# Turning attention probabilities on VectorE and moving them inside SBUF, in place of TensorE transposes

## The chip, the cores and the metric

The kernel runs on one core of a Trainium2 chip. The metric is the device time of one execution in microseconds. Engines are named TensorE (PE in the profile, with its weight loads as PEld), VectorE (DVE), ScalarE (ACT), GpSimd (POOL) and SyncE (SP), which issues DMA transfers. SBUF has 128 partitions; PSUM has eight banks of 512 float32 columns on each.

## The reference

One layer of a hybrid decoder over 4096 new tokens (and a small batch of 64 sample tokens), model width 1024, all in float32:

```
h = rmsnorm(x) ; z = h @ w_in                       # one projection, split among three head groups
A: silu(g) * B * conv3(C * h)                       # gated short convolution, 256 channels
B: window attention, 128 keys back, 8 query heads on 2 key heads, width 64,
   softmax with one learned sink logit per head, in blocks of 128 queries, * silu(g)
C: attention of 4 heads into 256 memory tokens, softmax, * silu(g)
y = concat(A, B, C) @ w_out ; out = x + rmsnorm(y)
```

For one block of 128 queries, B has 8 matrices of probabilities (queries x the 128 live keys: each query sees keys of its own block up to itself and keys of the block before beyond itself, so 128 columns hold both parts), and C has 4 heads x 2 halves of 128 memory keys. To multiply probabilities by values, TensorE needs them with the keys on the partitions; the softmax leaves them with the queries there.

## The kernel before, in words

**The projection** (`input_projection`) comes first, about 950 us. It multiplies blocks of 520 tokens in three phases, by a scheme of seven products, and stores queries, keys (`qd`), values (`vd`, transposed: features by tokens) and gates (`md`) in DRAM. Its third phase also runs small jobs (`third_jobs`), among them the memory keys and the whole attention of groups 0 and 1 (`early_scores`, `early_transposes`, `early_values`), the first 256 tokens.

**The attention stage** goes over 32 blocks of 128 tokens, `blocks[i]`, and a block of sample tokens near the end. `Block.run` makes the output product of block i: two halves of 512 columns, y0 and y1 (`p` 0 and 1), each 24 matmuls (8 slices x 3 passes of a float32 split into parts `mh` and `ml`). Between the slices it calls what `events_of(i)` has put at (half, slice):

- at (0, 0) `values_and_scores(i)`: scores of group i+3 (`scores`: window scores into four PSUM banks, memory scores into two), values of group i+1 (`values`: probabilities times values, into one two-bank PSUM tile `pv`, then two gate products on VectorE, `cross_gate` and the one at the end of `values`, in place in `mix`), and the softmax of group i+3;
- also there, the load `xr` of block i+2's residual input; at (0, 1) in even blocks `chunk_load`, keys and queries of a chunk of two blocks, issued by GpSimd; in odd blocks `load_mix`, 1 MB of gates;
- at (1, 0) `transposes(i)`: eight window matrices (`band_transposes`, TensorE into PSUM, copied out by ScalarE, masked twice per half by GpSimd's `affine_select` into `pv` and `pt`) and eight memory matrices (`cross_transposes`, copied out by VectorE and ScalarE); in even blocks also two transposes of the chunk's values (`Chunk.values`);
- at (1, 3) `split` of block i+1: ScalarE's cast `mh`, VectorE's difference `ml`.

After each half VectorE scales it (`yn`) and ScalarE squares and sums it; after both, the norm factor `yst` (VectorE, then a power on GpSimd), VectorE's product with the residual (`xr`), and the store `o_yp`, issued by SyncE. In the softmax, ScalarE copies the live half of the scores to SBUF, VectorE puts the other block's keys in their place (`copy_predicated`), takes the maximum, and ScalarE does eight exponentials with their sums; VectorE divides. The memory softmax reads PSUM, and GpSimd divides.

**What sets the order.** Every engine runs its own queue in order. In the projection's first two phases the order is the program's (`manual_schedule`). In the attention stage a planner orders the queues by its own cost estimates, apart from instructions marked `keep_in_program_order`. SyncE's transfers take eight semaphores in turn; a transfer waits until the one eight before it has landed. `yn` has one buffer, `xr` two: the load of a block's `xr` waits until the store of the block two before it has landed. `sm` and `xp`, the probabilities, have one buffer for odd groups and share three for even ones. Output halves lie in PSUM banks 0 and 5.

Of the kernel before, what the change touches and what calls it, by code (L numbers as in the profile page):

```python
# [51 lines left out]
def hybrid_layer(ctx: ExitStack, tc: tile.TileContext, a: dict):  # L52
    nc = tc.nc
    TE, V, S, G, DMA = nc.tensor, nc.vector, nc.scalar, nc.gpsimd, nc.sync
# [26 lines left out]
    vd = tc.dram_tile([P, NT], F32, name="vd")  # L81
    md = tc.dram_tile([KT, P, NT], F32, name="md")
# [711 lines left out]
    def third_jobs(b, p):  # L794
# [19 lines left out]
        if n > 13 and third["chunk"]:  # L814
            jobs.append(third["chunk"].pop(0))
        elif n > 13 and len(chunks) == 1:
            jobs.append(lambda: (chunk_load(1), chunks[1].load_values()))
        elif n > 13 and early[0] < 4 and n >= 38:
            if early[0] == 0:
                groups[2] = Group(chunks[1], 0)  # L820
            jobs.append(lambda u=early[0]: groups[2].early_scores(u))
            early[0] += 1
        return jobs

    early = [0]

    def first_chunk():
# [5 lines left out]
        chunk.load_values()  # L833
        chunk.load_mix()
        third["chunk"] = [lambda: chunk.values(None)]
# [66 lines left out]
    def input_projection():  # L902
        for i, (ph, b, p) in enumerate(steps):
# [36 lines left out]
            if ph == 2 and b == last:  # L940
# [4 lines left out]
                if p == 6:  # L945
                    jobs.append(blocks[0].split)
# [35 lines left out]
    def open_attention():  # L982
# [7 lines left out]
        vp = ctx.enter_context(tc.tile_pool(name="vp", bufs=5, side="right"))  # L990
# [40 lines left out]
    class Chunk:  # L1031
# [19 lines left out]
        def load_values(self):  # L1051

            self.vT = self.pool().tile([P, CT], F32, tag="vT", name=f"vT{self.c}")
            DMA.dma_start(self.vT, vd[:, self.ts])

# [14 lines left out]
        def values(self, vt_prev, pv=None):  # L1070

            self.vts = [vt_prev]
            ts = [psum(0, f"vtp{self.c}_{i}")[:, 0:P] if pv is None else pv[:, P * i : P * i + P] for i in range(2)]
            for i in range(2):
                TE.transpose(ts[i], self.vT[:, i * P : i * P + P], ident)
            for i in range(2):
                if self.c == 0:
                    vt = third["vt"] if i else third["work"].tile([P, P], F32, tag="v", name="vt0_0", bufs=1)
                else:
                    vt = vp.tile([P, P], F32, tag="v", name=f"vt{self.c}_{i}")  # L1080
                S.mul(vt, ts[i], 0.5)
                self.vts.append(vt)

    class Group:


        def __init__(self, chunk, i):
            self.chunk, self.i, self.b = chunk, i, 2 * chunk.c + i
            self.pt, self.pv, self.xpt = {}, {}, {}

        def open_scores(self, n):
            b = self.b
            if n == 0:
                t = wp.tile([P, D], F32, tag="sm", name=f"sm{b}", bufs=1) if b % 2 and b > 1 else work(f"sm{b}")
                self.sm = t.rearrange("p (h k) -> p h k", h=8)
            if n == 3:
                t = wp.tile([P, D], F32, tag="p", name=f"xp{b}", bufs=1) if b % 2 and b > 1 else work(f"xp{b}")
                self.p = t.rearrange("p (h j k) -> p h j k", h=2, j=2)

        def early_scores(self, n):  # L1100
# [3 lines left out]
            elif n == 2:  # L1104
                self.band_softmax()
            else:
                self.crosses([psum(0, f"xs{self.b}_{u}").rearrange("p (j k) -> p j k", j=2) for u in range(2)])

        def scores(self):
# [4 lines left out]
            self.bands(bands[:2], 0)  # L1114
            self.bands(bands[2:], 1)
            self.crosses(cross)

# [14 lines left out]
        def crosses(self, banks):  # L1132
            for j in range(2):
                self.both_rows([banks[u][:, j] for u in range(2)], self.chunk.q[:, j, :, self.i * P : self.i * P + P], third["mk"][:, :, j])
            for u in range(2):
                self.cross_softmax(banks[u], u)

        def band_out(self, s3, half, kvh):
            to = self.sm[:, 4 * kvh + 2 * half : 4 * kvh + 2 * half + 2, :]
            S.copy(to, s3[:, :, P : 2 * P])  # L1140
            V.copy_predicated(to, third["wmask"], third["negs"].unsqueeze(2).to_broadcast([P, 2, P]) if self.b == 0 else s3[:, :, 0:P])  # L1141

        def band_softmax(self):
# [3 lines left out]
            V.tensor_reduce(mx, sm, axis=AX.X, op=ALU.max)  # L1147
            V.scalar_tensor_tensor(nm, mx, -SCALE, third["nsink"], op0=ALU.mult, op1=ALU.min)  # L1148
            V.tensor_tensor(es, nm, third["sink"], op=ALU.add)
            S.activation(es, es, AF.Exp)  # L1150
            for h in range(n):
                S.activation(sm[:, h, :], sm[:, h, :], AF.Exp, bias=nm[:, h : h + 1], scale=SCALE, accum_out=den[:, h : h + 1])  # L1152
            V.tensor_tensor(den, den, es, op=ALU.add)  # L1153
            V.reciprocal(rd, den)
            V.tensor_tensor(sm, sm, rd.unsqueeze(2).to_broadcast([P, n, P]), op=ALU.mult)

        def cross_softmax(self, s, hh):
            p = self.p[:, hh]
# [490 lines left out]
```

## Time and profile before

| | us |
|---|---|
| median of 3 runs | 1551.4 (1550.34 to 1551.58) |
| the profiled execution | 1549.0 |
| its span, first to last instruction | 1547.3 |
| TensorE busy | 1525.7 |
| VectorE busy | 1124.6 |
| ScalarE busy | 776.8 |
| GpSimd busy | 335.6 |

The profile is one execution. A page gives busy times and the chain of work that ended last; queries give windows (busy time of every engine in a stretch), groups (instructions of one line with count, busy time, mean, and the idle time before them), the timeline, and waits. Matmuls are pipelined, so the time a matmul costs is the distance to the next one's start. SyncE has no busy time; its rows show when a transfer was issued and how long the issue took. In a TensorE row, `wt<-ident,sm` reads: wt is written, from ident and sm.

### The profile page before, as it was taken

The numbers are of one execution on the slowest core, as the hardware profiler recorded it, in microseconds if no ns is written. First come the engines' busy times: TensorE is split into PE (matmuls) and PEld (weight loads), VectorE is DVE, ScalarE is ACT, GpSimd is POOL, SyncE is SP. The second block draws the span as 40 slices with busy tenths as digits, with TensorE's granted clock in tenths as the row PEclk, the third lists the DMA queues.
The fourth block names the chain that finished last, engine by engine and source line by source line (L and its number), as shares of the span: only waits on it lengthen the run. The fifth ranks groups of instructions, "written<-read, shape, count | busy, mean of one in ns | idle before, by whom it ended". The sixth has DMA issues, their size and how long they took to land.

```text
span 1547.3 us, 30906 instructions
## 1 busy us (share of the span) xinstructions
PE 1525.7 (99%) x11981; PEld 1400.8 (91%) x11981; DVE 1124.6 (73%) x1850; ACT 776.8 (50%) x1964; POOL 335.6 (22%) x522
## 2 busy tenths in 40 slices
PE   9999999999999999999999998999999999999998
PEld 9999999999999999999999997788888888888776
DVE  6779888897988777996776678566666666666654
ACT  6776566475222222344454445555555555555541
POOL 0323323220400000000000101343333434334320
PEclk9999999999999999999999999999999999999999
DMA  9979999877755333669666859744554544445432
GB/s 260 212 204 257 262 274 266 276 243 269 198 179 179 125 125 126 215 209 304 234 216 199 255 189 299 219 145 137 143 161 147 150 137 137 137 137 160 153 107 96
DMA packets 169735, 299.47 MB, mean 194 GB/s; under 512 B 29813, under 2 KB 99445, under 8 KB 169557
## 3 DMA queue, kind: packets, MB, share of 16 engines
q1 hardware_dynamic: 128069, 226.69, 46.1%
q0 software_dynamic: 40800, 69.76, 16.9%
q8 instruction: 94, 1.54, 0.4%
q10 hardware_dynamic: 720, 1.05, 0.2%
q14 instruction: 52, 0.43, 0.1%
HBM read 190.38 MB, written 108.05 MB: 193 GB/s over the span
## 4 chain that ended last, share of the span: by engine, by line
PE 88%; DVE 4%; issue 3%; DMA 2%; ACT 2%; POOL 1%; SPq 0%; DVEq 0%; POOLq 0%; ACTq 0%
PE c L359 49%; PE y L1471 24%; PE pv L1017 5%; PE ws L1017 3%; PE xt L1207 2%; PE xs L1017 2%; PE wt L1194 2%; PE mem_acc L775 1%; DMA wor<-in_w_out 1%; ACT sm L1152 1%; DMA vd<-v 1%; DVE z L366 0%; DMA wr_2A<-in_w_in 0%; DVE wo L182 0%; POOL md L163 0%
## 5 line engine op out<-in xcount | busy, mean ns | idle before, releaser
L1471 PE MATMUL y<-wo,mh 128*128 128x512 f32 (+1 forms) x1040 | 338.6, 396 | 4.6 <-ACT y L1479 3.3
L366 DVE TENSOR_TENSOR z<-c,z 128x520 f32<-128x520 f32 (+1 forms) x308 | 194.7, 645 | 96.8 <-PE c L359 95.7
L1471 PEld LDWEIGHTS y<-wo,mh 128*128 128x128 f32 x1040 | 195.5, 189 | 56.3 <-DVE sm L1141 10.8
L1471 PE MATMUL y<-wo,ml 128*128 128x512 f32 (+1 forms) x520 | 202.5, 390 | 2.7 <-DVE ml L1450 2.7
L1471 PEld LDWEIGHTS y<-wo,ml 128*128 128x128 f32 x520 | 98.5, 189 | 20.8 <-DVE ml L1450 3.0
L1163 ACT ACTIVATE xp<-xs,xnm 128x256 f32<-128x256 f32 x128 | 59.5, 471 | 115.0 <-DVE xnm L1161 101.8
L1479 ACT ACTIVATE y<-y 128x512 f32<-128x512 f32 (+1 forms) x66 | 38.2, 578 | 130.8 <-DVE yn L1478 130.8
L1167 POOL TENSOR_SCALAR xp<-xp,xrd 128x256 f32<-128x256 f32 x128 | 61.5, 491 | 181.8 <-DVE xnm L1161 111.9
L1152 ACT ACTIVATE sm<-sm,wnm 128x128 f32<-128x128 f32 x256 | 99.1, 388 | 3.0 <-DVE wnm L1148 3.0
L1199 POOL TENSOR_SCALAR_AFFINE_SELECT wpv<-wpt 128x512 f32<-128x512 f32 x62 | 62.4, 1018 | 115.5 <-ACT wpt L1195 109.8
L1153 DVE TENSOR_TENSOR wden<-wden,wes 128x8 f32<-128x8 f32 x32 | 5.3, 167 | 88.3 <-ACT sm L1152 88.3
L1478 DVE TENSOR_TENSOR yn<-y,gpost 128x512 f32<-128x512 f32 (+1 forms) x66 | 45.1, 684 | 27.1 <-PE y L1471 26.4
L1017 PEld LDWEIGHTS ws<-kst,q 64*128 64x128 f32 x768 | 48.3, 188 | 11.3 <-issue 10.5
L734 POOL MEMSET negs<- 128x1 f32 x1 | 0.1, 98 | 264.4 <-PE c L359 264.4
L1017 PE MATMUL ws<-kst,q 64*128 64x256 f32 x768 | 55.4, 290 | 0.0
L368 ACT COPY z<-c 128x520 f32<-128x520 f32 (+1 forms) x44 | 24.4, 554 | 55.5 <-PE c L359 52.9
L1201 POOL TENSOR_SCALAR_AFFINE_SELECT wpt<-wpt 128x512 f32<-128x512 f32 x64 | 40.3, 639 | 52.7 <-ACT wpt L1195 50.5
L1141 DVE COPY_PREDICATED sm<-wmask,ws 128x256 f32<-128x256 uint8 x124 | 48.0, 441 | 4.5 <-ACT sm L1140 3.2
L1485 POOL TENSOR_TENSOR yst<-yst,mhalf 128x1 f32<-128x1 f32 (+1 forms) x33 | 18.4, 557 | 151.0 <-DVE yst L1484 151.0
L1489 DVE SCALAR_TENSOR_TENSOR xr<-yn,yst,xr 128x1024 f32<-128x1024 f32 (+2 forms) x34 | 42.5, 1253 | 8.1 <-POOL yst L1485 8.1
L400 ACT CAST zh<-z 128x520 fp32r<-128x520 f32 x56 | 33.4, 624 | 29.7 <-DVE z L366 26.9
L1152 ACT ACTIVATION_READ_ACCUMULATOR sm<-sm,wnm 128x1 f32 x256 | 48.2, 188 | 0.0
(957 smaller groups left out, 5064.1 us busy)
## 6 DMA issues: line engine op xcount, KB each, us to landing
q<-qd POOLq DMA_DIRECT2D x32, 768.0 KB, 8.5
xr<-in_x_p SPq DMA_DIRECT2D x32, 512.0 KB
nat<-in_x_p SPq DMA_DIRECT2D x39, 416.0 KB
o_yp<-xr SPq DMA_DIRECT2D x31, 512.0 KB
md<-th POOLq DMA_DIRECT2D x48, 260.0 KB, 6.6
qd<-zh SPq DMA_DIRECT2D x48, 260.0 KB
qd<-z SPq DMA_DIRECT2D x48, 260.0 KB
place<-md SPq DMA_DIRECT2D x8, 1024.0 KB
```

The lines of the kernel that those rows point to most:

```text
L359: TE.matmul(bank[:, :HW], l, r, start=first and i == 0, stop=last and i == 3 * KH - 1)
L366: add = lambda dst, other: V.tensor_tensor(dst, c, other, op=ALU.add)
L1017: ins = TE.matmul(o, w, x, **kw)
L1141: V.copy_predicated(to, third["wmask"], third["negs"].unsqueeze(2).to_broadcast([P, 2, P]) if self.b == 0 else s3[:, :, 0:P])
L1152: S.activation(sm[:, h, :], sm[:, h, :], AF.Exp, bias=nm[:, h : h + 1], scale=SCALE, accum_out=den[:, h : h + 1])
L1163: S.activation(p[:, i, :], s[:, i, :], AF.Exp, bias=nm[:, i : i + 1], scale=SCALE, accum_out=den[:, i : i + 1])
L1167: G.tensor_scalar(p[:, i, :], p[:, i, :], rd[:, i : i + 1], 0.5, op0=ALU.mult, op1=ALU.mult)
L1199: G.affine_select(self.pv[u].rearrange("p (h q) -> p h q", h=4), p3, pattern=[[0, 4], [-1, P]], compare_op=ALU.is_gt, fill=0.0, base=0, ch ...
L1201: G.affine_select(p3, p3, pattern=[[0, 4], [1, P]], compare_op=ALU.is_ge, fill=0.0, base=0, channel_multiplier=-1)
L1471: TE.matmul(acc, self.hl[l][:, k], wo[k][c0 // 512][:, r, c0 % 512 : c0 % 512 + c1 - c0], start=j == 0, stop=j == passes * KT - 1)
L1478: V.tensor_tensor(yn[:m, c0:c1], acc[:m], gpost[:m, c0:c1], op=ALU.mult)
L1489: V.scalar_tensor_tensor(self.xr[:m, cs], yn[:m, cs], st[:m, 3:4], self.xr[:m, cs], op0=ALU.mult, op1=ALU.add)
```

## The change

It replaces TensorE's transposes of groups 2 to 31 and of the values of chunks 1 to 15.

1. *Layout.* The probabilities of a group lie as four stripes of 32 keys: `sm` as (stripe, head, 32), `xp` as (stripe, head, half, 32). Masked copies, exponentials and divisions write and read through that order. The factor 0.5 of the gate, which the values carried, goes into the window weights (one more small VectorE product).
2. *Turning.* VectorE transposes each 32x32 square of the 128x1024 tile in place (`V.transpose`). Then sixteen transfers issued by SyncE, each 32 partitions by 1 KB, bring the squares of each stripe to their keys' partitions in a second tile (`wt`, `xt`): 32 transfers a group.
3. *Masks.* Four `affine_select` on GpSimd, now on tiles laid out as (query square, head, 32), two into a second tile `wd`.
4. *Values.* In the projection's third phase eight loads, eight VectorE transposes and 32 stores put the values into DRAM with tokens as rows (`vn`); each block then loads its 128 rows (`half_load`).
5. *The output.* y1 now lies in the second bank of the `pv` tile. Its square, the norm factor, the residual product and the store (`scale`, `store`) run in the next block, between its score matmuls (`tail(0)`, `tail(1)`).
6. *VectorE's order.* In blocks 1 to 30 every VectorE instruction keeps the program's order (`InOrder`). The softmax of a group is cut into maxima (before `values`) and weights (after).
7. The turning of group i+3 stands at (1, 2) of block i, its masks at (0, 4) of block i+1, its values at block i+2. Block 0 does the turning of group 2 at its start.

```
+    class InOrder:
+        on = False
+        def __getattr__(self, name):
+            fn = getattr(nc.vector, name)
+            return (lambda *args, **kw: tc.keep_in_program_order(fn(*args, **kw))) if self.on else fn
+    V = InOrder()
...
+    def v_turn(k):
+        turned = temp(f"vq{k}")[:, :512]
+        V.transpose(turned, third.pop(("v", k)))
+        rows_of = vn[512 * k : 512 * k + 512, :].rearrange("(b i) d -> i b d", i=32)
+        for g in range(4):
+            ds = slice(32 * g, 32 * g + 32)
+            DMA.dma_start(rows_of[:, :, ds], turned[ds].rearrange("p (b j) -> p b j", j=32))
...
+    def half_load(n):
+        halves[n] = vp.tile([P, P], F32, tag="v", name=f"vh{n}")
+        DMA.dma_start(halves[n], vn[P * n : P * n + P, :])
...
             self.bands(bands[:2], 0)
+            tail(0)
             self.bands(bands[2:], 1)
+            tail(1)
             self.crosses(cross)
+            self.band_softmax()
...
-        def transposes(self):
-            for u in range(2):
-                self.pt[u], self.pv[u] = (wp.tile([P, 512], F32, tag=t, name=f"w{t}{self.b}_{u}") for t in ("pt", "pv"))
-                self.band_transposes(u, psum(1 + u, f"wt{self.b}_{u}"))
-            for u in range(2):
-                self.xpt[u] = wp.tile([P, 512], F32, tag="xpt", name=f"xpt{self.b}_{u}")
-                self.cross_transposes(u, psum(3 + u, f"xt{self.b}_{u}"))
+        def moved(self, squares, name):
+            tc.keep_in_program_order(V.transpose(squares, squares))
+            to = wp.tile([P, 4, 256], F32, tag=name, name=f"{name}{self.b}")
+            src = squares.rearrange("p (k n) -> p k n", k=4)
+            for g in range(4):
+                for k in range(4):
+                    DMA.dma_start(to[32 * k : 32 * k + 32, g], src[32 * g : 32 * g + 32, k])
+            return to
+        def masks(self):
+            w = self.w
+            self.wd = wp.tile([P, 2, 8, 32], F32, tag="wd", name=f"wd{self.b}")
...
+            keep(self.wd, w[:, 2:4], P, -1, 64, ALU.is_gt)
+            keep(self.wd[:64], w[:64, 0:2], 64, 1, 0, ALU.is_ge)
+            keep(w[:, 0:2], w[:, 0:2], P, -1, 0, ALU.is_gt)
+            keep(w[:, 2:4], w[:, 2:4], P, 1, 64, ALU.is_ge)
...
         if 2 <= i + 1 < 2 * NCH:
             groups.pop(i + 1).values()
         if g < 2 * NCH:
-            groups[g].band_softmax()
+            for u in range(2):
+                groups[g].cross_softmax(cross[u], u)
+            groups[g].band_weights()
+            for u in range(2):
+                groups[g].cross_weights(u)
...
-                    acc = psum((0, 5, 1)[p], f"y{b}_{p}")[:, : c1 - c0]
+                    acc = (values_psum(f"y{b}_1")[:, 1] if p == 1 else psum(p // 2, f"y{b}_{p}"))[:, : c1 - c0]
...
-        at(1, 0 if i else 2, transposes, i)
+        if i == 0:
+            at(0, 4, turn, 1, 2)
+        at(0, 4, turn, 2, i + 2)
+        if i > 0 and i + 3 < 2 * NCH:
+            at(0, 5, half_load, i + 3)
+        at(1, 2, turn, 0, i + 3)
+        at(1, 2, turn, 1, i + 3)
...
+        InOrder.on = 0 < i < 31
```

More of the change, by code (lines that the diff above doesn't have):

```diff
@@ L1261, in values_and_scores @@
         g = i + 3
-        if g < 2 * NCH:
+        if i == 0:
+            turn(0, 2)
+        if g >= 2 * NCH:
+            tail(0)
+            tail(1)
+        else:
             groups[g] = Group(chunks[g // 2], g % 2)
-            groups[g].scores()
+            cross = groups[g].scores()
         if 2 <= i + 1 < 2 * NCH:
@@ L1497, in hybrid_layer @@
     chunk_load(2)
-    chunks[2].load_values()
+    for n in range(1, 4):
+        half_load(n)
     blocks[0].load()
```

173 lines of the change are left out of this document (108 added, 65 removed).

## The prediction, before the run

> **What bounds the kernel now.** I read the page first (busy shares, then the chain that ended last), then the table of windows, then the timeline of one block of the attention stage, SyncE's timeline over ten blocks, and the groups of VectorE and GpSimd in those blocks.
>
> ```profile
> span 1547.3 us, 30906 instructions
> PE 1525.7 (99%) x11981; PEld 1400.8 (91%) x11981; DVE 1124.6 (73%) x1850; ACT 776.8 (50%) x1964; POOL 335.6 (22%) x522
> PE 88%; DVE 4%; issue 3%; DMA 2%; ACT 2%; POOL 1%; SPq 0%; DVEq 0%; POOLq 0%; ACTq 0%
> ```
>
> TensorE is busy 99% of the span and carries 88% of the chain. So work taken from TensorE shortens the kernel, as long as nothing else takes its place.
>
> ```profile
> 1105.13:1285.30 180.17, 180.17 (x1334) 146.85 (x1332) 115.06 (x241) 102.41 (x380) 69.43 (x106) 1.00 0.50 147
> ```
>
> This window (columns: TensorE, its weight loads, VectorE, ScalarE, GpSimd, clock, DMA share, GB/s) runs from one output store to the tenth after it: ten blocks in 180.17 us, 18.02 us a block. TensorE has no gap; VectorE is busy 11.5 us a block, ScalarE 10.2, GpSimd 6.9, and the DMA engines half the time.
>
> **What is taken from TensorE.** One even block in the timeline, its value matmuls (the first row) and its turning:
>
> ```profile
> 1103.85 1.09 PE L1017 MATMUL pv<-xpt,mv 128*64 128x128 f32 x16
> ...
> 1106.33 0.50 PE L1471 MATMUL y<-wo,mh 128*128 128x512 f32 x1
> ...
> 1111.47 0.39 PE L1471 MATMUL y<-wo,ml 128*128 128x512 f32 x1
> 1111.70 0.39 PE L1471 MATMUL y<-wo,mh 128*128 128x512 f32 x1
> 1111.93 0.38 PE L1075 MATMUL vtp<-ident,vT 128*128 128x128 f32 x2
> 1112.14 1.04 PE L1194 MATMUL wt<-ident,sm 128*128 128x128 f32 x8
> 1113.02 1.04 PE L1207 MATMUL xt<-ident,xp 128*128 128x128 f32 x8
> 1113.81 0.48 PE L1471 MATMUL y<-wo,mh 128*128 128x512 f32 x1
> ```
>
> The matmuls are pipelined, so a price is a distance between starts: all value matmuls into pv 2.5 us (1103.85 to 1106.33), an output matmul 0.23 (1111.47 to 1111.70), the two value transposes 0.21, the eight window transposes 0.88, the eight memory transposes 0.79.
>
> ```profile
> L1194 PE MATMUL wt<-ident,sm x256: 271/273/300, 799.7 to 1496.5; 128*128 128x128 f32 x128
> ```
>
> ```profile
> L1207 PE MATMUL xt<-ident,xp x256: 271/273/328, 820.7 to 1497.7; 128*128 128x128 f32 x128
> ```
>
> ```profile
> L1075 PE MATMUL vtp<-ident,vT x32: 270/272/274, 779.7 to 1475.9; 128*128 128x128 f32 x32
> ```
>
> Of 32 groups, 30 lose their sixteen transposes (groups 0 and 1 keep them), and 15 of 16 chunks lose two: 30 x 1.67 + 15 x 0.21 = 53.3 us. A block would fall from 18.02 to 16.24 us.
>
> **What TensorE gets in exchange.** The second output half y1 now lies in the second bank of the one pv tile. In the built order of the odd blocks from 5 to 27, and of blocks 1 and 4, TensorE runs all 24 matmuls of the first half, then the value matmuls into pv, then y1 at once. y1 must wait until VectorE has read pv by its two gate products. In most even blocks six matmuls of the first half (6 x 0.23 = 1.4 us) stand between and cover that.
>
> ```profile
> L1160 DVE TENSOR_REDUCE xmx<-xs 128x2 f32<-128x512 f32 x20 | 12.8, 681 | 0.0
> L1155 DVE TENSOR_TENSOR sm<-sm,wrd 128x1024 f32<-128x1024 f32 x10 | 12.2, 1224 | 0.3
> L1147 DVE TENSOR_REDUCE wmx<-sm 128x8 f32<-128x1024 f32 x10 | 12.1, 1211 | 0.0
> L1208 DVE COPY xpt<-xt 128x512 f32<-128x512 f32 x10 | 6.8, 680 | 0.0
> L1450 DVE TENSOR_TENSOR ml<-mix,mh 128x1024 fp32r<-128x1024 f32 x5 | 6.1, 1226 | 9.2 <-ACT mh L1447 9.2
> ...
> L1254 DVE TENSOR_TENSOR place<-place,pv 128x512 f32<-128x512 f32 x5 | 3.4, 682 | 0.0
> ...
> L1219 DVE TENSOR_TENSOR place<-place,pv 128x256 f32<-128x256 f32 x5 | 2.1, 414 | 0.0
> ```
>
> The gates take 0.41 + 0.68 = 1.1 us, rounded up to 1.2 for the signals between the engines: 14 blocks with 1.2 us of TensorE idle and block 3, with two matmuls between, some 0.7: 17.5 us back. The value matmuls now read their moving operand in runs of 32 columns, where the window ones read runs of 64 before; I take no change. The other end, a value matmul twice as dear, would cost 2.5 us a block and the whole gain.
>
> **VectorE.** A transpose of 128x1024 is not in the trace. The passes over 1024 columns cost 1.21 to 1.23 us, a product, a maximum or a subtraction; I take 1.22, and for the upper end twice that, as if the squares went through twice. Per block VectorE loses the xpt copy (0.68) and gains two transposes (2.44) and a small product (0.15, an estimate from the small rows): 11.5 - 0.7 + 2.6 = 13.4 us of a block of about 17. It fits, but its order is now fixed in blocks 1 to 30, so each of its waits holds everything behind it. The order runs: yn of y1; four masked copies and the output scaling; the 1.2 us maximum; the gates (wait for pv); the memory maxima; the window weights (wait for eight exponentials); yn of y0; both transposes (the second waits for GpSimd's scaling); ml; yn of y1. From the end of pv to yn of y0 the rows add to 0.41 + 0.68 + 2 x 0.68 + 1.22 + 0.68 (yn, 512 columns like the xpt copy) and about 1.2 of small ones, 5.5 us; the square after it frees the bank of the next scores about 6.3 us after pv. TensorE gets there 5.5 + 1.2 us after pv in an odd block (24 x 0.23, and the wait for the gates), 6.9 in an even one. The slack is 0.4 to 0.6 us. ml ends some 2 us into the next block, where y0 wants it 2.5 us in. With joints this tight I add 0.2 us a block, 29 x 0.2 = 6 us (between 0 and 0.5 a block).
>
> ScalarE only loses work (the copies out of wt, xt and vtp). GpSimd keeps four selections of 512 columns a group:
>
> ```profile
> L1199 POOL TENSOR_SCALAR_AFFINE_SELECT wpv<-wpt 128x512 f32<-128x512 f32 x20 | 21.0, 1060 | 30.5 <-ACT wpt L1195 30.5
> ```
>
> ```profile
> L1201 POOL TENSOR_SCALAR_AFFINE_SELECT wpt<-wpt 128x512 f32<-128x512 f32 x20 | 12.4, 632 | 0.7
> ```
>
> Two at 1.06 and two at 0.63 are 3.4 us. For even groups they stand behind the scaling's power of the odd block (about 4.5 us in) and end near 7.9; the window products start near 9. Nothing is lost; if the masks slipped by over a microsecond, TensorE would pay what is over.
>
> **SyncE and the moves.** Each group adds 32 transfers of 32 rows by 1 KB. Their issues, and what else stands in SyncE's queue:
>
> ```profile
> 1105.13 0.34 SPq L1490 DMA_DIRECT2D o_yp<-xr  x1
> 1111.41 0.33 SPq L1433 DMA_DIRECT2D xr<-in_x_p  x1
> 1112.34 0.32 SPq L1054 DMA_DIRECT2D vT<-vd  x1
> 1119.34 0.37 SPq L1068 DMA_DIRECT2D place<-md  x1
> 1123.30 0.34 SPq L1490 DMA_DIRECT2D o_yp<-xr  x1
> 1127.09 0.33 SPq L1433 DMA_DIRECT2D xr<-in_x_p  x1
> ```
>
> ```profile
> 842.00 0.32 SPq L165 DMA_DIRECT2D qd<-z  x1
> 842.37 0.44 SPq L165 DMA_DIRECT2D qd<-zh  x1
> ```
>
> ```profile
> 1511.95 0.54 SPq L1433 DMA_DIRECT2D xr<-in_x_s  x1
> ```
>
> ```profile
> SPq L1433 <- DMA o_yp<-xr: 100.6, 24, 7.4
> ```
>
> An issue costs 0.31 to 0.37 us whether it moves 128 KB or 1 MB, and the next starts 0.37 us after it (842.00 to 842.37). I take 0.37 for a move, as no row falls with size; the other end is the 64-row load at 1511.95, 0.54 + 0.05 = 0.59. Below 0.37 there is nothing to gain, since TensorE is then the longer. SyncE's queue is in order, and xr waits there for the landing of the store before it (the wait row: 24 times, up to 7.4 us), 3.8 us after the store's issue in odd blocks (1123.30 to 1127.09) and 6.3 in even ones (1105.13 to 1111.41), when GpSimd's query loads are under way. In an odd block the queue holds that wait, xr (0.4), a value half (0.4) and 32 moves (11.8): 16.4 us. In an even block the half and three moves fall into the wait: 6.3 + 0.4 + 29 x 0.37 = 17.4, or 14.9 if the store, now issued later, meets no query loads. A pair of blocks takes SyncE 31.3 to 33.8 us; TensorE's pair is 2 x (16.24 + 0.2) + 1.2 = 34.1. So the moves just fit, and I cost them at nothing. They land 5 to 10 us into the block after their transposes, a good half block ahead of masks and products. If that cover goes, each 0.01 us more on a move costs 0.6 us a pair. The DMA engines' share rises from 0.50 by the moves' 1024 packets; at the dearer queue's average they add 1024 x 72 ns / 16 = 4.6 us to 9.0 in a block of 17, a share of 0.80:
>
> ```profile
> q0 software_dynamic: 9200, 9.83, 23.0%
> ```
>
> (9200 packets in 23.0% of 16 engines over the ten blocks.)
>
> **The rest.** The values are turned by eight VectorE transposes of 128x512 and written to DRAM by 32 small stores during the third phase of the projection:
>
> ```profile
> 800.00:900.00 100.00, 99.37 (x834) 94.66 (x833) 68.72 (x108) 43.99 (x87) 11.16 (x17) 1.00 0.68 223
> ```
>
> 8 x 0.68 us (the xpt copy's row, same size) lie beside a VectorE that is idle 31% there; zero, and 5 us if the evictions behind them come late. Block 0 must move group 2 within itself: 32 x 0.37 = 12 us of a block of 18; I take 2 us (0 to 5). The moved squares of y1 and the half loads issue beside running matmuls: zero.
>
> **The sum.** The profiled execution took 1549.0 us, 1.7 over its span and 2.4 under the median of the three runs. 1549.0 - 53.3 + 17.5 + 6 + 2 = 1521.2; against the median, 1523.6. I say 1523.
>
> **The rivals.**
>
> SyncE becomes the bound (slower). Mechanism: the moves' issue in SyncE's in-order queue. At 0.37 us a move the pair takes up to 33.8 us; before, a pair of blocks took 36.04. The 61 exposed issues reach that at 0.41 us a move with the long landing wait, 0.45 with the short one: from there on the change loses. At 0.48, midway between the two ends, a pair takes 38.0 to 40.5 and 14 pairs lose 28 to 63 us: 1580 to 1614. At 0.59 it passes 1650. For it: the 64-row row at 0.54 and other issues of 0.44; the built program also gives SyncE's transfers eight semaphores in turn, so a move waits until the eighth transfer before it has landed, and that can be the 512 KB xr load. Against: the many rows at 0.32 to 0.34. Chance 0.38. The Trainium skill, "DMA: Bandwidth & Descriptors", section Bandwidth, speaks for this rival: it says that transfers under 64 KB are dominated by their descriptors and should be batched to a megabyte. That the issue rows here do not fall with size agrees with it.
>
> VectorE becomes the bound (slower). There is a loop: ml lets y0 start, pv follows, pv lets VectorE go on to the next ml. From y0's start to pv's end TensorE needs 18 x 0.23 + 2.5 = 6.6 us in an even block and 8.0 in an odd one; from there VectorE needs 5.5 to yn of y0, two transposes and ml's 1.2. At 1.22 a transpose the loop takes 15.7 and 17.1 us, just inside TensorE's 16.24 and 17.4; at 2.44 it takes 18.2 and 19.6, 18.9 on average against 18.02 before, and 28 blocks lose 25 us: 1576. It decides from 1.98 us a transpose. For it: no row shows a transpose. Against: all passes over 1024 columns cost alike. Chance 0.10. The Trainium skill, "VectorE: DVE Perf Modes", section Rules for kernel authors, advises TensorE for a 128x128 transpose where PSUM will do, and so would keep the kernel as it was; the trace disagrees as far as TensorE is the full engine here, and no run yet shows VectorE's price.
>
> All joints hold and the gates are hidden: 1549.0 - 53.3 + 2, 1500 against the median. The built order of the odd blocks speaks against it. Chance 0.07.
>
> **How the numbers follow.** The forecast (1505 to 1545 by itself: stalls of 0 to 0.5 us a block, and 5 us each for block 0 and the projection) has 0.45. Below 1500 lies little; above 1600 lie the dearer half of SyncE's rival, 0.15. The range is 1498 to 1600. What a measurement of this kernel tells from no change is about 0.2%, 3 us. Faster: 0.45 + 0.07 + a little of the others, 0.53; same 0.03, where SyncE's rival crosses the old time; slower 0.44.
>
> **What would show it.** Right: no transposes on TensorE after group 1's; TensorE gaps of about 1.2 us before y1 in odd blocks, ended by VectorE's gates; blocks of 16.4 and 17.6 us; StreamTranspose near 1.22; SyncE's issues 0.37 apart. Wrong: TensorE waiting for a DMA before pv, or ScalarE's score copies for the lanes of old moves (SyncE's rival); ml or yn late with VectorE gapless (VectorE's rival).

## The result, and the profile after

The changed kernel takes 1814.9 us (median of 4 runs, 1812.16 to 1815.94), the kernel before 1550.9 us beside it (1549.02 to 1551.58). The ratio is 1.170, 95% interval 1.168 to 1.172: slower by 264 us, where 1523 was forecast.

The two windows below run from the scores of group 6 to those of group 26, 20 blocks each (columns as in the prediction: length, then busy time of TensorE, its weight loads, VectorE, ScalarE and GpSimd, granted clock, DMA share, GB/s). Before:

```profile
1011.11:1371.71 360.60, 360.50 (x2661) 293.70 (x2660) 230.13 (x480) 204.80 (x760) 138.94 (x210) 1.00 0.50 147
```

After:

```profile
1033.73:1549.11 515.38, 365.26 (x2321) 278.93 (x2320) 274.98 (x519) 174.61 (x680) 141.94 (x210) 0.86 0.51 143
```

A block went from 18.03 to 25.77 us. TensorE was full and now is busy 71%; no other engine in the row is above 54%, and the DMA engines are half idle. What is full has no column there: SyncE's queue. Its timeline over two blocks (at each "..." a row of moves or a value load is left out):

```profile
1301.43 0.53 SPq L1582 DMA_DIRECT2D o_yp<-xr  x1
...
1304.65 0.53 SPq L1516 DMA_DIRECT2D xr<-in_x_p  x1
...
1314.55 10.38 SPq L1244 DMA_DIRECT2D xt<-xp  x16
1325.02 0.53 SPq L1582 DMA_DIRECT2D o_yp<-xr  x1
1325.65 0.38 SPq L1090 DMA_DIRECT2D place<-md  x1
1331.32 0.34 SPq L1516 DMA_DIRECT2D xr<-in_x_p  x1
1331.75 0.38 SPq L1110 DMA_DIRECT2D vh<-vn  x1
1332.31 10.39 SPq L1244 DMA_DIRECT2D wt<-sm  x16
```

Sixteen moves take 10.4 us to issue. In two blocks the queue has only one pause, 5.3 us (1326.03 to 1331.32), where `xr` waits for the landing of the store `o_yp`; in the other block three moves and a value load are issued before `xr`, and it need not wait. Over the 20 blocks (columns of the tile rows: least, median and largest issue in ns; of the wait row: total us, times, longest):

```profile
L1244 SPq DMA_DIRECT2D wt<-sm x317: 507/589/1704, 1043.3 to 1549.0; - x159
```

```profile
L1244 SPq DMA_DIRECT2D xt<-xp x319: 512/589/1759, 1032.6 to 1531.8; - x160
```

```profile
SPq L1516 <- DMA o_yp<-xr: 55.7, 10, 6.4
```

From one move's start to the next it is 0.65 us (10.38 / 16). Per block that is 32 x 0.65 = 20.8 us, the other issues add 1.6 (0.53 + 0.38 + 0.34 + 0.38, in the block shown), the wait for the store 2.8 (55.7 / 20): 25.2 of 25.77 us. SyncE is the bound. TensorE shows where it is felt, in its waits over the same 20 blocks:

```profile
PE pv L1044 <- DMA xt<-xp: 69.4, 13, 9.0
PE pv L1044 <- DMA o_yp<-xr: 57.7, 7, 9.7
PE y L1554 <- DVE sm L62: 9.7, 15, 1.4
PE y L1554 <- DVE place L62: 6.9, 6, 1.3
PE y L1554 <- DVE mix L62: 6.3, 5, 1.3
```

127 us are spent ahead of the value products. They read the moves, and not the store that the second row names: in the block shown they start at 1330.67, before the store's landing lets `xr` go at 1331.32, and 5.7 us after the last move was issued (1314.55 + 10.38). Of the 265.5 us by which the profiled span grew (1547.3 to 1812.8), 155 lie in these 20 blocks (515.38 - 360.60). The stretch before them starts its count 22.6 us later (1033.73 against 1011.11), and the stretch behind them takes 88 us longer (263.69 against 175.59); the moves of the last eight groups are issued there, and the loads of the sample block stand in the same queue behind the moves (GpSimd's wait for `smraw`):

```profile
POOL smask L1446 <- DMA smraw<-in_smask: 35.8, 1, 35.8
```

### The profile page after: what moved, and what is told of

It reads as the page before. It is cut to its first block, busy times and chain, and to the rows that moved or that the text cites. A ratio compares the mean times of both kernels' runs of the same rounds, so it can differ in the third digit from the quotient of the medians.

```text
span 1812.8 us, 31491 instructions
## 1 busy us (share of the span) xinstructions
PE 1537.6 (85%) x11471; PEld 1380.1 (76%) x11471; DVE 1197.3 (66%) x1920; ACT 732.0 (40%) x1844; POOL 344.2 (19%) x522
## 5 line engine op out<-in xcount | busy, mean ns | idle before, releaser
L1044 PE MATMUL pv<-xt,mv 128*64 128x128 f32 x480 | 54.4, 398 | 176.6 <-DMA xt<-xp 108.8
L1044 PEld LDWEIGHTS pv<-xt,mv 128*64 128x64 f32 x480 | 43.9, 207 | 188.2 <-issue 181.8
L1195 ACT ACTIVATE sm<-sm,wnm 128x128 f32<-128x128 f32 x256 | 99.1, 389 | 116.9 <-DVE wnm L62 113.8
L62 DVE TENSOR_TENSOR mix<-mix,pv 128x256 f32<-128x256 f32 (+1 forms) x32 | 16.3, 551 | 159.0 <-PE pv L1044 153.8
L62 DVE TENSOR_TENSOR place<-place,pv 128x256 f32<-128x256 f32 (+1 forms) x28 | 14.3, 551 | 134.3 <-PE pv L1044 134.3
L1178 ACT COPY sm<-ws 128x256 f32<-128x256 f32 x128 | 41.2, 376 | 68.1 <-PE ws L1044 43.2
L1258 POOL TENSOR_SCALAR_AFFINE_SELECT wd<-wt 128x512 f32<-128x512 f32 (+1 forms) x60 | 60.8, 1013 | 32.0 <-DMA wt<-sm 16.5
L62 DVE SCALAR_TENSOR_TENSOR xr<-yn,yst,xr 128x1024 f32<-128x1024 f32 x30 | 42.8, 1427 | 21.1 <-POOL yst L1575 21.0
L1044 PE MATMUL pv<-wt,vh 128*64 128x256 f32 x240 | 53.0, 583 | 0.0
L283 ACT ACTIVATE nat<-nat 104x1024 f32<-104x1024 f32 x40 | 42.2, 1056 | 15.7 <-DMA nat<-in_x_p 15.7
```

Of the source, the lines that this page charges most:

```text
L62: return (lambda *args, **kw: tc.keep_in_program_order(fn(*args, **kw))) if self.on else fn
L283: S.activation(t[:RG], t[:RG], AF.Square, accum_out=r[:RG, i : i + 1])
L1044: ins = TE.matmul(o, w, x, **kw)
L1178: S.copy(to, squares(s3[:, :, P : 2 * P]))
L1195: S.activation(sm[:, h], sm[:, h], AF.Exp, bias=nm[:, h : h + 1], scale=SCALE, accum_out=den[:, h : h + 1])
L1258: G.affine_select(out, src, pattern=[[32 * sign, 2], [0, 8], [sign, 32]], compare_op=op, fill=0.0, base=base * sign, channel_multiplier=-s ...
```

## The experiments

The theory: one move takes about 0.65 us of SyncE's in-order queue, by the issue itself, and 32 of them a group are more than a block. The rivals: the moves' landing time before the products; the eight semaphores or other traffic slowing cheap issues; the written-out orders; VectorE.

**The price of an issue by itself.** Behind the kernel before, series of transfers of several shapes; the last 43 of them are issued when no engine computes.

```
+    pa_, pb_ = (probe.tile([P, 4, 256], F32, name=n) for n in ("pra", "prb"))
...
+    for g in range(4):
+        for k in range(4):
+            DMA.dma_start(pb_[32 * k : 32 * k + 32, g], pa_[32 * g : 32 * g + 32, k])
...
+            DMA.dma_start(pe_[32 * k : 32 * k + 32, g], pd_[32 * g : 32 * g + 32, k])
...
+            S.dma_start(pj_[32 * k : 32 * k + 32, g], pa_[32 * g : 32 * g + 32, k])
```

> The kernel before, with a series of transfers behind its last store, when no engine has anything else to do: 16 moves as the change makes them (32 rows by 1 KB, SBUF to SBUF, other partitions), 16 transfers of 128 rows by 256 B inside SBUF, 16 of 32 rows from DRAM, 8 of 64 rows and 4 of 128 rows inside SBUF on equal partitions, 4 of 32 rows by 4 KB, 8 moves issued by ScalarE, 4 stores of 32 rows by 4 KB to DRAM and one load of 512 KB. Theory (the issue of such a move is dear by itself on SyncE): the 16 moves are issued 0.55 to 0.70 us apart here too, 0.65 in the kernel after. Rival (an issue costs the 0.37 us that I took, and in the kernel the moves wait for the landing of the eighth transfer before them, or are slowed by other traffic): the first seven or eight moves are issued 0.3 to 0.4 us apart, and only the later ones are longer. The other shapes say what the price hangs on: rows, SBUF or DRAM, or the issuing engine.

SyncE's timeline at the end, after all other work: `prc` 128 rows by 256 B inside SBUF, `pre` 32 rows from DRAM (`prd`), `prf` 64 rows, `prh` 128 rows by 1 KB and `pri` 32 rows by 4 KB inside SBUF, `prk` stores to DRAM, `prl` the 512 KB load.

```profile
1559.02 3.75 SPq L1556 DMA_DIRECT2D prc<-pra  x6
1562.81 7.77 SPq L1560 DMA_DIRECT2D pre__19014<-prd  x16
1570.63 4.96 SPq L1564 DMA_DIRECT2D prf<-pra  x8
1575.63 2.53 SPq L1567 DMA_DIRECT2D prh<-pra  x4
1578.21 2.50 SPq L1570 DMA_DIRECT2D pri<-pra  x4
1580.75 2.05 SPq L1577 DMA_DIRECT2D prk<-pra  x4
1584.65 0.39 SPq L1579 DMA_DIRECT2D prl<-prk  x1
```

The moves as in the change ran a little earlier, beside the last stores; the eight from ScalarE's queue too:

```profile
L1552 SPq DMA_DIRECT2D prb<-pra x16: 507/589/1685, 1524.7 to 1539.4; - x16
```

```profile
L1574 ACTq DMA_DIRECT2D prj<-pra x8: 517/607/1317, 1523.8 to 1529.4; - x8
```

The move's median is 589 ns here as in the kernel. Inside SBUF a transfer in a series takes 0.62 to 0.63 us (3.75 / 6, 4.96 / 8, 2.53 / 4, 2.50 / 4) whether it has 32, 64 or 128 rows and 32 or 128 KB; with DRAM at one end it is 0.49 (7.77 / 16) and 0.51 (2.05 / 4); alone in the queue, with DRAM at one end, 0.39. As far as these shapes tell, the price hangs on both ends being SBUF and on standing behind another transfer, not on size, other work or the engine that issues. The shape of the rival, cheap first moves and dear later ones, is not there: the least of the sixteen is 507 ns.

**No moves at all.** VectorE writes the squares into the tile that is read.

```
-            tc.keep_in_program_order(V.transpose(squares, squares))
             to = wp.tile([P, 4, 256], F32, tag=name, name=f"{name}{self.b}")
-            src = squares.rearrange("p (k n) -> p k n", k=4)
-            for g in range(4):
-                for k in range(4):
-                    DMA.dma_start(to[32 * k : 32 * k + 32, g], src[32 * g : 32 * g + 32, k])
+            tc.keep_in_program_order(V.transpose(to.rearrange("p k n -> p (k n)"), squares))
             return to
```

> The kernel after, but VectorE writes the turned squares straight into the tile that the products read, and no transfer spreads them: the values are taken from the wrong partitions, so the attention's output is not the reference's. All else stays: 2 transposes a group, the written-out order, y1 in pv's second bank, the values turned in the projection. Theory (SyncE's queue alone makes the change slow): 1505 to 1545 us, the sum of the prediction with the moves at nothing; TensorE's gaps in a pair of blocks come to 1 to 2 us. Rival (the written-out order, or the loop between ml, pv and VectorE, makes it slow): above 1600 us, with TensorE waiting for VectorE.

1502.6 us, ratio to before 0.966 (0.963 to 0.969), 2 us under the range expected. Its window of the same 20 blocks:

```profile
1022.04:1340.97 318.93, 318.93 (x2321) 254.06 (x2321) 279.86 (x520) 170.12 (x680) 136.91 (x210) 1.00 0.57 166
```

15.95 us a block with TensorE full at clock 1.00. So all 312 us between this and the kernel after come with the moves, through the queue or through what the planner does because of them; the runs below tell the two apart. And the wait before y1 is gone: with the moves out of the program, and nothing else changed, the planner put the value products ahead of y0:

```profile
1293.13 1.69 PE L1044 MATMUL ws<-kst,q 64*128 64x256 f32 x24
1294.66 0.88 PE L1044 MATMUL xs<-mk,q 64*128 64x256 f32 x12
1295.47 1.09 PE L1044 MATMUL pv<-xt,mv 128*64 128x128 f32 x16
1296.39 1.03 PE L1044 MATMUL pv<-wt,vh 128*64 128x256 f32 x8
1297.36 0.66 PE L1044 MATMUL pv<-wd,vh 64*64 64x256 f32 x8
1297.95 0.50 PE L1550 MATMUL y<-wo,mh 128*128 128x512 f32 x1
```

All 24 matmuls of y0 now cover the gates.

**Half the moves.** The window squares move, the memory squares are written straight.

```
+            if name == "xt":
+                tc.keep_in_program_order(V.transpose(to.rearrange("p k n -> p (k n)"), squares))
+                return to
```

> The kernel after, with the 16 moves of the window weights kept and the 16 of the memory weights left out (turned straight into the tile that is read, so the memory attention is not the reference's). Theory (SyncE's issue time is the bound): 16 x 0.65 = 10.4 us a block beside 4 to 5 us of other issues and the wait for a store to land is 15 to 17 us a block, at or just under TensorE's 17: 1510 to 1570 us, no longer 26 us a block. Rival (each group of moves costs its landing time before the products, whatever the queue has to issue): the window weights still come late, and the time falls by half of the loss or less: 1660 us or above.

1566.1 us, ratio 1.007 (1.004 to 1.010); in the expected range, near its upper end. 20 blocks take 377.43 us, 18.87 each, in turns of about 16 and 22. SyncE's timeline has 10 us of moves a block, and ahead of them now in every block the wait for the store (a row of the timeline, and the waits of the 20 blocks):

```profile
1304.62 10.18 SPq L1247 DMA_DIRECT2D wt<-sm  x16
```

```profile
SPq L1519 <- DMA o_yp<-xr: 116.9, 20, 6.8
```

The 16 moves taken out bring 249 of the 312 us, and the other 16 cost 64. With about 1.5 us of other issues the queue holds 10.2 + 1.5 + 5.8 (116.9 / 20) = 17.5 of the 18.87 us, still more than TensorE's 15.95. So the loss does not fall evenly with the number of moves: what the queue needs beyond TensorE's block, 1.6 us, is over half of the 2.9 us that a block is longer than without moves. The rest is not traced.

**Moves issued, but not waited for by TensorE.** The value products read a constant tile: the window products as shown, the memory products in the same way.

```
-                    tiled(out(o[cs, n]), halves[...][:, cs], heads(self.w[:, 2 * n : 2 * n + 2], kvh), ...
+                    tiled(out(o[cs, n]), halves[...][:, cs], heads(fixed[:, 2 * n : 2 * n + 2], kvh), ...
```

> The kernel after with all its 32 moves a group issued and the masks made on them, but TensorE's value products read a constant tile in their place, so that no product waits for a move (the attention's output is not the reference's). Theory (the pace of SyncE's queue is the bound, and the wait of TensorE before the products is only where it shows): the time stays within 3% of the kernel after, 1760 to 1815 us, and TensorE or ScalarE waits elsewhere, for the lanes of old moves or for the loads and stores behind them in the queue. Rival (the latency of the last moves on the path to the products is what costs): 1510 to 1580 us.

1816.0 us, ratio 1.167 (1.163 to 1.172), 1 us above the range expected and the kernel after's to 0.1%. With the wait before the products removed the time is the same; the wait moved (stretch from 1100 to 1700 us):

```profile
ACT sm L1178 <- DMA wt<-sm: 228.0, 11, 22.8
PEld y L1555 <- DVE sm L62: 194.2, 11, 19.9
```

ScalarE cannot write the next scores before the moves have left the tile, and through VectorE this holds TensorE. The landing before the products is not the cause; the pace of the queue is.

**The orders.** Three runs left the moves' number alone or took them out, and changed only orders. First VectorE's order given back to the planner (`InOrder.on = False`), with the moves:

> The kernel after, with the written-out order of VectorE left to the planner; the moves stay. The planner also places TensorE's work another way (the value products within the next block's scores). Theory (SyncE's queue is the bound, and the order on VectorE and TensorE matters little beside it): 1770 to 1860 us. Rival (the written-out order holds VectorE's transposes back, and with them the moves): below 1700 us.

1782.8 us, ratio 1.150 (1.146 to 1.153). Then the orders of TensorE and GpSimd written out besides VectorE's, with the moves:

```
-                        TE.matmul(acc, ...
+                        ins = TE.matmul(acc, ...
+                        if 0 < b < 31 and p == 0 and j == 0:
+                            tc.keep_in_program_order(ins)
...
-                G.tensor_tensor(st[:m, 3:4], st[:m, 3:4], mhalf[:m, 0:1], op=ALU.pow)
+                power = G.tensor_tensor(st[:m, 3:4], st[:m, 3:4], mhalf[:m, 0:1], op=ALU.pow)
+                if 0 < b < 31:
+                    tc.keep_in_program_order(power)
```

> The kernel after with its 32 moves a group, and the two orders of the run before: value products ahead of y0 on TensorE, masks ahead of the power on GpSimd. Theory (SyncE's queue is the bound, and no order of the other engines can mend it): 1770 to 1850 us. Rival (the places of products and masks made the loss, since the planner counted on late moves): below 1700 us.

1839.8 us, ratio 1.184 (1.180 to 1.187). Both lie in the ranges expected of a full queue. The orders move the time by 32 us down and 25 up, against 264: they are not what made the loss. Without moves, VectorE's order given to the planner:

> The run without moves, with VectorE's order left to the planner (the attention is not the reference's). TensorE's order is the same in both. Theory (the written-out order is no part of the loss, and its worth is small): 1490 to 1520 us. Rival (the written-out order is what keeps the gates and transposes in time): above 1530 us, TensorE waiting for VectorE.

1523.7 us, ratio 0.980 (0.976 to 0.984), 21 us more than with the order written out, and a little above what I expected; the same 20 blocks take 336.67 us, 16.83 each. So the written-out order is a gain, once TensorE is the bound: 0.88 us a block.

**VectorE at twice the price.** Each square is turned twice (the edit is shown against the run without moves).

```
+            tc.keep_in_program_order(V.transpose(squares, squares))
             tc.keep_in_program_order(V.transpose(to.rearrange("p k n -> p (k n)"), squares))
```

> The run without moves, with each of VectorE's two transposes a group done twice (once in place, once into the tile that is read; the attention is not the reference's). It is the price of 2.44 us a transpose that I had as the far end. VectorE was busy 87.6 us of 100 in the run without moves, 13.97 us a block of 15.95; 2.5 us more make 16.45. Theory of the prediction (VectorE becomes the bound from 1.98 us a transpose): the blocks get longer, 0.5 us if VectorE can close all its gaps, 2.5 us if it keeps them: 1515 to 1575 us, with TensorE waiting for VectorE. Rival (VectorE has more room than that, since the products' place in TensorE's order opened the loop): within 6 us of the run without moves.

1532.2 us, ratio 0.988 (0.985 to 0.991). That is in the range of the theory. A block takes 17.03 us (340.55 / 20), 1.08 more than without moves, for two more transposes; VectorE is busy 2.1 us a block longer, and now 94%:

```profile
1021.37:1361.92 340.55, 320.31 (x2321) 254.00 (x2320) 321.28 (x561) 172.09 (x680) 128.86 (x210) 1.00 0.54 155
```

**By way of DRAM: fewer, larger transfers.** Four stores and one load in place of 16 moves.

```
+            bd = tc.dram_tile([4, P, 256], F32, name=f"bd{name}{self.b}")
             for g in range(4):
-                for k in range(4):
-                    DMA.dma_start(to[32 * k : 32 * k + 32, g], src[32 * g : 32 * g + 32, k])
+                DMA.dma_start(bd[g].rearrange("(k j) n -> j k n", k=4), src[32 * g : 32 * g + 32])
+            self.back.append((to, bd))
+            if name == "xt":
+                for t, d in self.back:
+                    DMA.dma_start(t, d.rearrange("g p n -> p g n"))
```

> The kernel after, with the 16 moves of a tile replaced by four stores of 32 rows by 4 KB to DRAM and one load of 512 KB back, which put the squares where the moves put them: 10 transfers a group for SyncE instead of 32, twice the bytes. In the probe these stores were issued in 0.45 us and the load in 0.39: 8 x 0.45 + 2 x 0.39 = 4.4 us a group, where the moves took 20.8. The planner places the value products behind all of y0 here, so y1 (in pv's second bank) should wait for VectorE's gates in every block: 28 x 1.26 = 35 us over the run without moves. Theory (SyncE's issue time was the loss): 1525 to 1550 us. Rival (it is the traffic inside SBUF and the DMA engines' load, or the landing of what is moved): the second landing and the doubled bytes make it no better, above 1650 us.

1566.6 us, ratio 1.010 (1.007 to 1.013): 248 us of the loss are gone, but it is 17 us above the range expected. In its timeline each block has two waits of TensorE for VectorE, and the second I had not counted:

```profile
1302.52 0.47 PE L1558 MATMUL y<-wo,mh 128*128 128x512 f32 x1 [1.26 <-DVE mix L62]
...
1311.16 0.50 PE L1558 MATMUL y<-wo,mh 128*128 128x512 f32 x1 [0.57 <-DVE sm L62]
```

1.26 before y1 and 0.57 before y0, which the trace puts down to VectorE's masked copies: 1.83 of the 2.10 us that its block is longer than without moves (361.04 / 20 - 15.95). Then with the value products ahead of y0 on TensorE (the first part of the diff in "The orders"):

> The run before this one, and besides the first matmul of y0 is held behind the value products in TensorE's written-out order, as TensorE's order was in the run without moves. Theory (y1's wait is a matter of where the value products stand, not of pv's second bank by itself): no wait before y1, 1500 to 1515 us. Rival (the squares that come by way of DRAM land too late for products that stand half a block earlier): TensorE waits for a DMA or for GpSimd's masks before pv, 1530 us or above.

1577.8 us, ratio 1.018 (1.014 to 1.022): slower, not faster. The waits before y1 and y0 are gone, but in every second block TensorE waits for the masks:

```profile
1320.01 1.38 PE L1044 MATMUL pv<-wt,vh 128*64 128x256 f32 x8 [2.90 <-POOL wt L1262]
```

```profile
1316.26 0.57 POOL L1581 TENSOR_TENSOR yst<-yst,mhalf 128x1 f32<-128x1 f32 x1 [5.45 <-DVE yst L62]
1316.81 2.36 POOL L1262 TENSOR_SCALAR_AFFINE_SELECT wd<-wt 128x512 f32<-128x512 f32 x2
1319.23 1.40 POOL L1262 TENSOR_SCALAR_AFFINE_SELECT wt<-wt 128x512 f32<-128x512 f32 x2
```

GpSimd sat idle for 5.45 us ahead of the small power, and the masks stood behind that. Neither side of what I expected was right. The theory's cause was: the order on TensorE does take the y1 wait away; its time was not. The rival's time and its wait for the masks came, but for another reason than late squares, as the next run shows. With the power held behind the masks (the second part of that diff):

> The run with the value products ahead of y0 and the squares by way of DRAM; besides, GpSimd's small power of the output's scale is held behind the masks of the same block in its written-out order. In the earlier run TensorE waited 2.9 us in every second block for the masks, which stood behind that power on GpSimd and so behind the scores of the next block. Theory (the masks' place in GpSimd's queue was the wait, not the landing of the squares): 1500 to 1520 us, faster than the kernel before and than the one after, no wait before the value products in the even blocks. Rival (the squares land too late by way of DRAM): 1550 us or above, GpSimd's masks waiting for a DMA.

1524.1 us (5 runs), ratio 0.981 (0.979 to 0.984): faster than the kernel before by 1.9%, than the one after by 291 us, a few us above the range expected. Its 20 blocks:

```profile
1018.34:1340.02 321.68, 319.38 (x2323) 253.96 (x2322) 273.82 (x520) 170.12 (x680) 143.95 (x211) 1.00 0.98 295
```

16.08 us a block, TensorE full, though the DMA share is now 0.98. The profiled span is 17.6 us longer than without moves (1519.9 against 1502.3). All of that lies behind these blocks: from the scores of group 26 to the end it takes 179.88 us, without moves 161.33; the 20 blocks add 2.8, and the start is 3.7 shorter. Behind them the sample block's loads stand again behind stores and loads of the last groups, and GpSimd waits for one of them:

```profile
POOL smask L1450 <- DMA smraw<-in_smask: 14.2, 1, 14.2
```

That this wait makes the 18.6 us is read from the trace and was not tried.

## Why the prediction was wrong, step by step

**SyncE and the moves: the step that failed.** I took 0.37 us for a move and let the far end of the bound be 0.59. It is 0.65. So the moves did not just fit and could not be costed at nothing. The structure of the sum held: an odd block with the store's wait in the open, an even one where three moves stand ahead of `xr`. Put 0.65 into its own formula, and the pair takes 33.8 + 61 x 0.28 = 50.9 us; measured are 51.5 (2 x 25.77). That they agree so closely is partly luck: from the store's issue to `xr` it is 6.3 us in the odd block (1325.02 to 1331.32) and 3.2 in the even one (1301.43 to 1304.65), where I had 3.8 and 6.3, so two errors nearly cancel. The term that failed is the price of a move, and the reading of the rows behind it was wrong: I saw that issues do not differ by size, which holds, and concluded that a move costs what any row costs. The rows at 0.32 to 0.37 were issues alone in the queue, with DRAM at one end. The row at 842.37, right behind another issue, was 0.44, and the series in the probe says why that was the row to look at: a transfer behind another is dearer, and one inside SBUF dearer again. The bound of 0.59 was not a bound either, since no row that I used had both ends in one memory. The trace of the kernel before has two such rows, copies from DRAM to DRAM near its end, right behind another issue:

```profile
1529.70 0.60 SPq L1420 DMA_DIRECT2D o_kc<-in_cwk_nat  x1
1530.35 0.58 SPq L1421 DMA_DIRECT2D o_vc<-in_cwv_nat  x1
```

They start 0.65 us apart, which is the price that the moves turned out to have.

**The rival came true, above its price.** SyncE as the bound had 0.38, with 0.48 us a move and 1580 to 1614 us. At 0.65 the pairs lose 14 x (50.9 - 36.04) = 208 us; the rest of the 264 is the start and the end, which the rival did not price. The range ended at 1600, near that mid price; the dearer half had 0.15 and lay outside, and the range missed by over 200 us. Of the signs that I named for this rival the first came, TensorE waiting for a DMA before pv (127 us in the 20 blocks). ScalarE's score copies waited only 9 us for moves there (4.9 + 4.2), but 228 us where the products did not wait. The eight semaphores, which I gave as one reason for it, are not needed: all waits of the moves in SyncE's queue sum to 6.5 us over the 20 blocks, and a move's issue has the same median at the kernel's end, in the probe. The Trainium skill, "DMA: Bandwidth & Descriptors", section Bandwidth, which I had beside this rival, advises to batch small transfers. The runs agree with the advice: 16 moves made into five transfers a tile take 248 us off. They do not show the page's reason, the descriptors, since 32 rows and 128 cost the same to issue. In the section "Issuing engines are not separate DMA queues" the same page of the Trainium skill calls the time to initiate a transfer usually small relative to the transfer itself. Here it is the bound: 20.8 us of issue a block, in which the DMA engines are busy about half the time.

**TensorE's gain: right, a little low.** The block without transposes and without moves is 15.95 us; I had 16.24. 2.08 us a block are gained, 1.78 were counted; the 0.3 between them are not traced further.

**y1 in pv's second bank: the price was right, the cover was not.** The wait is 1.26 us where it stands (1.2 forecast). In the kernel after it costs nothing that shows: with the products ahead of y0 that kernel is no faster (1839.8 us), as SyncE sets its pace; in the first run by way of DRAM it costs its 1.26 us in every block, and another 0.57 before y0; with the products ahead of y0, nothing. It depends on where the planner puts the products, and that depends on when it expects the moves.

**VectorE: right.** The rows of the kernel after:

```profile
L62 DVE STREAM_TRANSPOSE xp<-xp 128x1024 f32<-128x1024 f32 x20 | 24.9, 1246 | 3.5 <-POOL xp L1220 3.5
L62 DVE STREAM_TRANSPOSE sm<-sm 128x1024 f32<-128x1024 f32 x20 | 24.7, 1235 | 0.0
```

1.24 us against 1.22, and 13.7 us a block (274.98 / 20) against 13.4. Its rival was priced too high (and by its own terms it begins at 2.01 us a transpose, (18.02 - 14.0) / 2, not at 1.98): at the double price the loop was to take 18.9 us a block; it takes 17.03, in the order with the products ahead of y0. The Trainium skill, "VectorE: DVE Perf Modes", section Rules for kernel authors, prefers TensorE for a 128x128 transpose; here, where TensorE is full, VectorE with cheap enough moves is 1.9% faster, and with dear ones 17% slower.

**The rest.** GpSimd's masks take 2 x 1.06 + 2 x 0.72 = 3.6 us (3.4 forecast); that they cost nothing holds only for a good place in GpSimd's queue, as the 2.9 us waits showed. The DMA engines' work grows by 0.51 x 25.77 - 0.50 x 18.03 = 4.1 us a block (4.6 forecast), but over a longer block, so the share stays 0.51 and not 0.80. The values turned in the projection cost nothing that shows: in the 290 us up to 950 TensorE is busy 285.85 us before and 286.58 after. The start was far too low: I had 2 us, 5 at most. In the 50 us from 950 on, TensorE loses 15.6 us, and 9.4 of that without any moves (before, after, and without moves):

```profile
950.00:1000.00 50.00, 43.93 (x311) 35.15 (x312) 31.53 (x62) 24.02 (x88) 17.89 (x27) 0.93 0.80 232
```

```profile
950.00:1000.00 50.00, 28.31 (x172) 21.43 (x171) 24.18 (x47) 13.80 (x58) 11.08 (x15) 0.78 0.73 200
```

```profile
950.00:1000.00 50.00, 34.55 (x239) 28.66 (x239) 36.04 (x66) 22.83 (x74) 10.89 (x15) 0.83 0.84 253
```

The end, where the sample block's loads stand behind moves, was not in the sum.

With the moves out of it, the change does better than the sum: the span falls by 45.0 us (1547.3 to 1502.3), where the sum had 27.8. In the 20 blocks it is 41.7 (360.60 - 318.93) against 20 x (1.78 - 0.2) - 10 x 1.2 = 19.6: no waits before y1, no loose joints, 0.3 us more gained a block. At the start it is worse: the scores of group 6 come 10.9 us later (1022.04 against 1011.11).

## What to carry to other kernels

A queue that only issues transfers has no busy time in the table of engines, and can be the bound while every engine in that table is half idle: count its issues per block, price them by a row of the same kind (where both ends lie, and whether it stands in a series), sought in the whole trace, and add the landings that it waits for. If no such row exists, the dearest row at hand is no upper bound, and the range should reach what the change costs beyond it. Few large transfers by a longer way can beat many short ones, and then the places of the neighbours in the in-order queues decide whether the gain arrives. Sharing the moves between two engines' queues, the nearest other remedy, was not tried.

## What the runs showed of the hardware that I had not expected

An issue of SyncE costs 0.32 to 0.39 us alone, 0.49 to 0.51 in a series with DRAM at one end, 0.62 to 0.65 in a series inside SBUF, with 32 rows as with 128, and much the same from ScalarE's queue (607 ns median against 589). The two copies from DRAM to DRAM in the kernel before, at 0.60 and 0.58, cost as much, so what counts may be that both ends lie in one memory; more such rows were not tried. Behind moves even an ordinary store takes 0.53 instead of 0.34 us.

TensorE that waits a few microseconds a block is granted less clock: 0.86 over the 20 blocks of the kernel after, against 1.00 before, and in such a block eight value matmuls take 1.95 us that took 1.03 in the run without moves (its row is in the timeline above). They stand behind a wait of 9.4 us, and the value products run at a granted clock of 0.50:

```profile
1332.40 1.95 PE L1044 MATMUL pv<-wt,vh 128*64 128x256 f32 x8
```

```profile
1330.67:1335.35 4.68, 4.68 (x33) 2.84 (x33) 0.00 (x0) 0.00 (x0) 0.00 (x0) 0.50 0.90 302
```

That this is no loss of its own here, as SyncE sets the pace, is argued and was not tried.

The moves inside SBUF left the DMA engines at 0.51; the way by DRAM brings them to 0.98, and TensorE still keeps 16.08 us a block. How much is left before they become the bound was not tried.
